# Two-layer hybrid decoder trunk: the first layer's normalised input from a column-wise copy of x instead of from transposes

## The chip, the cores and the metric

One core of one Trainium2 chip. Its engines are TensorE (PE, matrix products; PEld is its loading of weights), VectorE (DVE), ScalarE (ACT) and GpSimd (POOL); SyncE (SP) issues most DMA loads. The metric is device microseconds (us) of one execution, the median of several runs.

## The reference

Two layers of a decoder trunk, 256 positions, width 1024, float32. What matters here is how each layer begins, and what runs beside it:

```python
for l in range(DEPTH):                                  # DEPTH = 2
    h = rms_norm(x, norm_g[l])                          # x * rsqrt(mean(x*x) + eps) * g, per position
    proj = h @ w_in[l]                                  # 1024 -> 5120 columns
    q_a, k_a, v_a, q_h, f_h, i_h, q_m, z = split(proj)
    o_a = causal attention of 8 heads (QK norm, partial rotary) on q_a, k_a, v_a
    o_h = rms_norm(gated linear recurrence(q_h, f_h, i_h))
    kv_m = rms_norm(mem, mem_norm_g[l]) @ w_mem_kv[l]   # 256 memory tokens, 1024 -> 1024 columns
    o_m = attention of q_m on kv_m
    y = concatenate([o_a, o_h, o_m]) * silu(z)
    x = x + y @ w_out[l]
```

## The kernel before

**Precision.** Every large product is done as three: each operand is split in a high part (a cast to the format fp32r) and the remainder, so that the weights are `wh` and `wl`, the normalised input `hTh` and `hTl` (both in the tile `hT`, 8 blocks k of 128 columns, each with 256 positions high and 256 low), the memory tokens `mTh` and `mTl`.

**Weights.** All weights come in chunks of 128x1024 float32 (512 KB) through four buffers `wr`, loaded by SP in the order of use: 8 of `w_mem_kv`, 40 of `w_in`, 12 of `w_out`, and again for the second layer. ACT casts a chunk to `wh` (L201, or L205 where a gain is multiplied in) and DVE subtracts to get `wl` (L215, L219); each has three buffers. PE's products are at L262 (`mm`) and L266 (`mm_row`, kept in program order).

**Order.** The program is written as a main line of matmul groups; between their parts it steps generators (`g_norm`, `g_km`, `g_mem_r`, ...) that issue the other work. From this a scheduler makes one fixed list of instructions for each engine, which the engine works in order; what is marked with `keep_in_program_order` isn't moved.

**The first stage.** The main line begins with `group_kv`, the product of the memory tokens with `w_mem_kv`, chunks c0 to c7; its key half is finished first, then its value half. The memory tokens come already as columns (`mem_t`, put so on the host), and rows of them (`memr`) come as well, only for the squares of their norm (`g_mem_r`, L442 on ACT); the factor `rm` is applied after the product. `g_km` copies the key half out of PSUM (`kn`, L624 on DVE for one half of the positions and L625 on ACT for the other) and goes on to its norm (`sq`, `ssk`, `rk`).

**The layer's input.** Beside that product `g_norm(0)` makes `hT` from the rows `xs`: squares on ACT (L459), the factor `r` (`msx` on DVE, `rx` on POOL), two scalings `xn` on DVE (L467), 16 transposes of 128x128 on PE (L475, a product with the unit matrix `ident`) into four PSUM tiles `sd`, and from there eight times a cast with the gain on ACT (L483, 128x256) and a subtraction on DVE (L484). Then comes `group_a`, whose first products (the forget gate) read `wh` and `hT`, both parts of one k at a time, in the order of k. `g_norm(1)` does the same for the second layer.

Of the kernel before, what the change touches and what calls it, by code (L numbers as in the profile page):

```python
# [22 lines left out]
D = 1024  # L23
# [22 lines left out]
def hymba_kernel(ctx: ExitStack, tc: tile.TileContext, x, mem, mem_t, positions, w_in, w_out, w_mem_kv,  # L46
# [17 lines left out]
    def room(what, n=1):  # L64
        while held[what] + n > room_of[what]:
            yield
# [97 lines left out]
    def load(dst, src):  # L164
        tc.keep_in_program_order(nc.sync.dma_start(dst, src))
# [211 lines left out]
    dma_to(8)  # L377
    for t in range(2):
        load(memr[t], dram(mem, t * 128 * D, [[D, 128], [1, D]]))
# [74 lines left out]
    def g_norm(l):  # L454
# [11 lines left out]
        for t in range(2):  # L466
            nc.vector.tensor_scalar(xn[t], xs[:, t], r[:, t:t + 1], None, op0=OP.mult)  # L467
        yield 3
        for kp in range(4):
            yield from room("sd")  # L470
            pt = side_tile()
            for j in range(2):
                k = kp * 2 + j
                for t in range(2):
                    ins = nc.tensor.transpose(pt[:, j * 256 + t * 128:j * 256 + (t + 1) * 128],  # L475
                                              xn[t][:, k * 128:(k + 1) * 128], ident)
                    if l == 0:
                        tc.keep_in_program_order(ins)
            for j in range(2):
                k = kp * 2 + j  # L480
                c = GR_NORM + 8 * l + k
                src = pt[:, j * 256:(j + 1) * 256]
                nc.scalar.activation(hTh[:, k], src, AF.Copy, scale=gT[:, c:c + 1])  # L483
                nc.vector.scalar_tensor_tensor(hTl[:, k], in0=src, scalar=gT[:, c:c + 1],  # L484
                                               in1=hTh[:, k].bitcast(F32), op0=OP.mult, op1=OP.subtract)
            rel()
            if kp % 2 == 1:
                yield
# [110 lines left out]
    for tag, n, bufs in (("PTh", 1792, 1), ("PTl", 1792, 1), ("hX", 512, 1), ("qk", 1024, 1), ("sq", 512, 2),  # L599
                         ("vmh", 1024, 1), ("vml", 1024, 1), ("kmh", 1024, 1), ("kml", 1024, 1), ("as", 512, 2),  # L600
                         ("al", 256, 2), ("hF", 1024, 1), ("sg", 512, 2), ("ih", 1024, 1),
                         *((f"y{c}{br}", 1024, 1) for br in (H_, A_, M_) for c in "hl"), ("hT1", 512, 1), ("blk", 1536, 1)):
# [156 lines left out]
    def y_tiles(br):  # L759
        if f"y{br}" not in T:  # L760
            T[f"y{br}"] = [sb.tile([128, 4, 256], F32R, name=f"y{c}{br}", tag=f"y{c}{br}", bufs=1) for c in "hl"]
        return T[f"y{br}"]
# [595 lines left out]
```

## Time and profile before

| what | value |
|---|---|
| runs | 391.07 to 391.2 us, median 391.19 us (3 runs) |
| profiled execution | span 389.4 us from its first to its last instruction; no time of its own is given beside it |
| PE busy | 383.4 us (98%), mean granted clock 0.999 |
| DVE / ACT / POOL busy | 320.7 / 247.8 / 84.4 us |
| bytes moved | 84.48 MB, mean 217 GB/s |
| all transposes to `hT`, both layers (L475) | 32 instructions |

The time of a run is about 1.8 us above the span, for what lies around the program. A PE matmul record shows its latency too, so that records overlap; the distance from start to start is what one costs. The kernel's stage in question lies between about 14 us, when the squares of x begin, and 36 us, when the first two chunks of `w_in` are used up.

### The profile page before, as it was taken

What the parts mean: (1) busy time and instruction counts of PE and PEld (TensorE: products, weight loads), DVE (VectorE), ACT (ScalarE), POOL (GpSimd) and SP (SyncE); (2) the same over time, 40 slices, a digit from 0 to 9 for tenths busy, and PEclk for the clock granted to TensorE, in tenths of its full rate; (3) what the DMA queues carried; (4) which work ended last, traced back from release to release, by engine and by line L of the source; (5) the groups of instructions that cost most, each with busy time, mean ns of one, the idle gap of its engine ahead of it and who ended that gap; (6) DMA issues with size and microseconds to landing.
All of it is one profiled execution on the core that took longest, in us unless ns stands there. A gap on an engine that the chain in (4) does not pass through costs nothing.

```text
span 389.4 us, 6794 instructions
## 1 busy us (share of the span) xinstructions
PE 383.4 (98%) x2455; PEld 319.5 (82%) x2455; DVE 320.7 (82%) x621; ACT 247.8 (64%) x414; POOL 84.4 (22%) x129
## 2 busy tenths in 40 slices
PE   8999999999999999999999999999999999999996
PEld 5888888788788888778888888888888888877885
DVE  4789899999659999967577689899696799997663
ACT  5988755567768849464375756445765984885540
POOL 3004400534102522500000040014061063152000
PEclk9999999999999999999999999999999999999999
DMA  7986595539534889985464568636765179999512
GB/s 257 418 312 190 185 312 180 163 111 320 176 107 150 272 277 337 309 269 176 158 205 164 175 204 260 226 109 195 238 198 185 54 266 278 335 275 291 184 47 108
DMA packets 26241, 84.48 MB, mean 217 GB/s; under 512 B 3552, under 2 KB 5984, under 8 KB 26208
## 3 DMA queue, kind: packets, MB, share of 16 engines
q1 hardware_dynamic: 22304, 71.31, 54.5%
q0 software_dynamic: 3616, 12.59, 10.7%
q8 instruction: 19, 0.31, 0.3%
q10 hardware_dynamic: 288, 0.15, 0.1%
q14 instruction: 14, 0.11, 0.1%
HBM read 74.60 MB, written 9.44 MB: 216 GB/s over the span
## 4 chain that ended last, share of the span: by engine, by line
PE 90%; DVE 3%; DMA 3%; ACT 2%; issue 1%; SPq 0%; DVEq 0%; ACTq 0%
PE acc L262 62%; PE acc L1244 17%; PE sd L262 5%; PE sd L266 4%; DMA wr<-in_w_out_dram 2%; DMA wr<-in_w_mem_kv_dram 1%; ACT P L1169 1%; PE sd L475 1%; ACT wh L201 1%; DVE wl L215 1%; DVE wl L219 1%; DVE blk L1185 1%; DVE yl L186 1%; PE sd L1000 0%; PE sd L1130 0%
## 5 line engine op out<-in xcount | busy, mean ns | idle before, releaser
L201 ACT CAST wh<-wr 128x1024 fp32r<-128x1024 f32 x96 | 100.7, 1050 | 69.3 <-PE acc L262 49.3
L215 DVE TENSOR_TENSOR wl<-wr,wh 128x1024 fp32r<-128x1024 f32 x96 | 117.0, 1219 | 26.3 <-ACT wh L201 26.1
L262 PE MATMUL acc<-wh,hT 128*128 128x512 f32 x384 | 122.9, 394 | 0.0
L262 PEld LDWEIGHTS acc<-wh,hT 128*128 128x128 f32 x384 | 71.5, 188 | 15.8 <-issue 0.7
L262 PE MATMUL acc<-wl,hT 128*128 128x512 f32 x192 | 75.6, 394 | 0.0
L262 PE MATMUL acc<-hT,wh 128*128 128x512 f32 x256 | 64.7, 392 | 0.0
L262 PEld LDWEIGHTS acc<-hT,wh 128*128 128x128 f32 x256 | 46.0, 189 | 8.4 <-ACT kn L625 0.4
L262 PEld LDWEIGHTS acc<-wl,hT 128*128 128x128 f32 x192 | 36.1, 188 | 7.3
L219 DVE SCALAR_TENSOR_TENSOR wl<-wr,gT,wh 128x1024 fp32r<-128x1024 f32 (+1 forms) x29 | 31.1, 1097 | 10.2 <-ACT wh L205 10.1
L1244 PE MATMUL acc<-wl,yh 128*128 128x512 f32 (+1 forms) x96 | 37.4, 390 | 0.7 <-DVE wl L219 0.7
L1244 PE MATMUL acc<-wh,yl 128*128 128x512 f32 (+1 forms) x96 | 37.2, 388 | 0.0
L262 PEld LDWEIGHTS acc<-hT,wl 128*128 128x128 f32 x256 | 34.9, 190 | 2.5
L205 ACT ACTIVATE wh<-wr,gT 128x1024 fp32r<-128x1024 f32 (+1 forms) x29 | 28.3, 1000 | 13.4 <-PE acc L1244 5.2
L262 PE MATMUL acc<-hT,wl 128*128 128x256 f32 x256 | 35.7, 282 | 0.0
L1244 PE MATMUL acc<-wh,yh 128*128 128x512 f32 (+1 forms) x96 | 33.1, 392 | 0.0
L262 PE MATMUL acc<-wh,mTh 128*128 128x512 f32 x64 | 25.5, 402 | 0.7 <-ACT wh L205 0.4
L262 PE MATMUL acc<-wh,mTl 128*128 128x512 f32 x64 | 25.0, 394 | 0.0
L965 POOL TENSOR_TENSOR rka<-msa,pw 128x8 f32<-128x8 f32 x4 | 9.9, 2477 | 58.2 <-DVE msa L964 58.2
L1051 ACT ACTIVATE P<-P,nba,rq 128x128 f32<-128x128 f32 (+1 forms) x32 | 17.1, 535 | 8.3 <-DVE nba L1045 8.3
L1244 PEld LDWEIGHTS acc<-wl,yh 128*128 128x128 f32 x96 | 18.0, 188 | 4.8 <-DVE wl L219 1.3
L1244 PEld LDWEIGHTS acc<-wh,yh 128*128 128x128 f32 x96 | 18.0, 188 | 4.2 <-issue 0.7
L1244 PEld LDWEIGHTS acc<-wh,yl 128*128 128x128 f32 x96 | 18.0, 188 | 3.6
(219 smaller groups left out, 589.0 us busy)
## 6 DMA issues: line engine op xcount, KB each, us to landing
wr<-in_w_in_dram SPq DMA_DIRECT2D x80, 512.0 KB, 4.1
wr<-in_w_out_dram SPq DMA_DIRECT2D x24, 512.0 KB, 5.2
wr<-in_w_mem_kv_dram SPq DMA_DIRECT2D x15, 512.0 KB, 4.3
there<-blk POOLq DMA_DIRECT2D x4, 768.0 KB, 6.3
PT<-there POOLq DMA_DIRECT2D x16, 192.0 KB, 4.6
there<-blk POOLq DMA_DIRECT2D x6, 512.0 KB, 5.2
there<-blk SPq DMA_DIRECT2D x4, 512.0 KB, 2.9
P<-there POOLq DMA_DIRECT2D x16, 128.0 KB, 6.5
```

The source lines that it names most:

```text
L186: T["DVE"] = nc.vector.tensor_tensor(lo, a, h.bitcast(F32), op=OP.subtract)
L201: nc.scalar.copy(whs[i], raws[i])
L205: nc.scalar.activation(whs[i][:, sl], raws[i][:, sl], AF.Copy, scale=gT[:, g:g + 1])
L215: nc.vector.tensor_tensor(wls[i], raws[i], whs[i].bitcast(F32), op=OP.subtract)
L219: ins = nc.vector.scalar_tensor_tensor(wls[i][:, sl], in0=raws[i][:, sl], scalar=gT[:, g:g + 1], in1=whs[i][:, sl].bitcast(F32), op0=OP.mu ...
L262: nc.tensor.matmul(o, lhsT=a, rhs=b, start=s, stop=e)
L266: tc.keep_in_program_order(nc.tensor.matmul(o, lhsT=a, rhs=b, start=s, stop=e))
L475: ins = nc.tensor.transpose(pt[:, j * 256 + t * 128:j * 256 + (t + 1) * 128], xn[t][:, k * 128:(k + 1) * 128], ident)
L965: nc.gpsimd.tensor_tensor(r[:, t8], ms[:, t8], pw[:, :8], op=OP.pow)
L1051: nc.scalar.activation(P[:, i, kc[t]], P[:, i, kc[t]], AF.Exp, bias=nb[:, c:c + 1], scale=rq[:, r:r + 1], accum_out=sm[:, c:c + 1])
L1169: T["exp"] = nc.scalar.activation(P[:, t, i], ps[t][:, i * 256:(i + 1) * 256], AF.Exp, bias=nb[:, c:c + 1], scale=r[:, cr:cr + 1], accum_o ...
L1244: ins = nc.tensor.matmul(a, lhsT=y, rhs=wt[:, cs], start=n == (0 if to is None else nk - 2) and j == 0, stop=n == nk - 1 and j == 2)
```

## The change

The host hands over x a second time, as `x_t`: 128 partitions are the 128 columns of a block, and along them stand 8 strips of 32 positions with the 8 blocks k in each. Two loads of 512 KB bring it into the tile `xT` on SP's queue, ahead of those of `memr`. In the first layer `g_norm` now leaves out `xn` and the transposes. It copies the factor `r` of each position across 128 columns (`rc`, DVE); two products of `rc` with `ident` put the factors of all 256 positions on every partition (`rb`, PSUM); eight instructions on DVE scale `xT` by gain and factor in place; and for each half of the k, ACT casts 128x1024 to `hTh` and DVE subtracts 128x1024 to `hTl`. `xT` shares its place with the recurrence's output tiles, which become one tile for that. The second layer is as before.

```diff
+    xT = sb.tile([128, 8, 8, 32], F32, name="xT", tag=f"y{H_}", bufs=1)
+    for t in range(2):
+        load(xT[:, 4 * t:4 * t + 4].rearrange("p q k i -> p (q k i)"),
+             dram(x_t, t * 128 * D, [[D, 128], [1, D]]))
     for t in range(2):
         load(memr[t], dram(mem, t * 128 * D, [[D, 128], [1, D]]))
...
         nc.gpsimd.tensor_tensor(r, ms, pw[:, :2], op=OP.pow)
         yield
-        for t in range(2):
-            nc.vector.tensor_scalar(xn[t], xs[:, t], r[:, t:t + 1], None, op0=OP.mult)
-        yield 3
-        for kp in range(4):
...
+        if l == 0:
+            rc = sb.tile([128, 2, 128], F32, name="rc", tag="sq", bufs=2)
+            nc.vector.tensor_copy(rc, r[:, :, None].to_broadcast([128, 2, 128]))
+            yield 2
+            rb = side_tile()
+            for t in range(2):
+                mm_row(rb[:, t * 128:(t + 1) * 128], rc[:, t], ident)
+            rb3 = rb[:, :256].rearrange("p (q i) -> p q i", i=32)
+            yield
+            for k in range(8):
                 c = GR_NORM + 8 * l + k
-                src = pt[:, j * 256:(j + 1) * 256]
-                nc.scalar.activation(hTh[:, k], src, AF.Copy, scale=gT[:, c:c + 1])
-                nc.vector.scalar_tensor_tensor(hTl[:, k], in0=src, scalar=gT[:, c:c + 1],
-                                               in1=hTh[:, k].bitcast(F32), op0=OP.mult, op1=OP.subtract)
+                nc.vector.scalar_tensor_tensor(xT[:, :, k], in0=xT[:, :, k], scalar=gT[:, c:c + 1], in1=rb3,
+                                               op0=OP.mult, op1=OP.mult)
+                if k % 4 == 3:
+                    ks = slice(k - 3, k + 1)
+                    src = xT[:, :, ks].rearrange("p q k i -> p k q i")
+                    hi, lo = (a[:, ks].rearrange("p k (q i) -> p k q i", i=32) for a in (hTh, hTl))
+                    nc.scalar.copy(hi, src)
+                    nc.vector.tensor_tensor(lo, src, hi.bitcast(F32), op=OP.subtract)
+                    yield
             rel()
...
+    def strips(a):
+        return a.reshape(2, 4, 32, 8, 128).transpose(0, 4, 1, 3, 2)
```

The lists of the engines change with it. ACT's list before, from the last squares of the memory tokens to the casts of the first chunks of `w_in` (`wh<-wr`, L201):

```order
L483 ACTIVATE hT<-sd,gT 128x256 x3
L442 ACTIVATE memr,ssm<-memr 128x1024
L483 ACTIVATE hT<-sd,gT 128x256 x3
L201 CAST wh<-wr 128x1024
L483 ACTIVATE hT<-sd,gT 128x256 x2
L201 CAST wh<-wr 128x1024
L625 COPY kn<-acc 128x512
L665 ACTIVATE vmh<-acc,rm 128x512
```

And now, from the first half of `hT` on (the first square of `memr` stands just ahead in both lists):

```order
L487 CAST hT<-xT 128x4x256
L446 ACTIVATE memr,ssm<-memr 128x1024
L649 COPY kn<-acc 128x512
L487 CAST hT<-xT 128x4x256
L635 ACTIVATE sq<-kn 128x512
L201 CAST wh<-wr 128x1024
L635 ACTIVATE sq<-kn 128x512
L201 CAST wh<-wr 128x1024
```

The first cast of `w_in` has moved from ahead of `kn` to behind `kn`, the last of `hT` and the first `sq`.

DVE's list before, from the last three remainders of the memory weights to the first of `w_in`:

```order
L219 SCALAR_TENSOR_TENSOR wl<-wr,gT,wh 128x1024 x3
L484 SCALAR_TENSOR_TENSOR hT<-sd,gT,hT 128x256 x3
L445 TENSOR_SCALAR msm<-ssm 128x2
L448 RECIPROCAL rm_159<-msm 128x2
L449 TENSOR_SCALAR rm_159<-rm_159 128x2
L484 SCALAR_TENSOR_TENSOR hT<-sd,gT,hT 128x256 x3
L215 TENSOR_TENSOR wl<-wr,wh 128x1024
L624 COPY kn<-acc 128x512
```

And now:

```order
L219 SCALAR_TENSOR_TENSOR wl<-wr,gT,wh 128x1024 x3
L481 SCALAR_TENSOR_TENSOR xT<-xT,gT,sd 128x8x32 x8
L648 COPY kn<-acc 128x512
L488 TENSOR_TENSOR hT<-xT,hT 128x4x256
L449 TENSOR_SCALAR msm<-ssm 128x2
L452 RECIPROCAL rm_162<-msm 128x2
L453 TENSOR_SCALAR rm_162<-rm_162 128x2
L488 TENSOR_TENSOR hT<-xT,hT 128x4x256
L636 TENSOR_REDUCE ssk<-sq 128x4
L215 TENSOR_TENSOR wl<-wr,wh 128x1024
```

`kn` now stands ahead of both subtractions of `hT`, and a reduction over `sq` ahead of the first remainder of `w_in`. On PE the two products of `rc` stand ahead of chunk c5, where the 16 transposes stood in two groups near its end; further on, in the first half of the first layer, small instructions of the rotary tables and the recurrence change places with their neighbours on DVE and ACT, and POOL's lists differ in one place (four copies for the rotary tables, behind the masks now).

More of the change, by code (lines that the diff above doesn't have):

```diff
@@ L45, in hymba_kernel @@
 @with_exitstack
-def hymba_kernel(ctx: ExitStack, tc: tile.TileContext, x, mem, mem_t, positions, w_in, w_out, w_mem_kv,
+def hymba_kernel(ctx: ExitStack, tc: tile.TileContext, x, x_t, mem, mem_t, positions, w_in, w_out, w_mem_kv,
                  gains, moba_g, out):
@@ L465, in g_norm @@
         yield
[L466 to L488 removed]
+        if l == 0:
[8 more added lines that the diff above has]
+            for k in range(8):
+                c = GR_NORM + 8 * l + k
+                nc.vector.scalar_tensor_tensor(xT[:, :, k], in0=xT[:, :, k], scalar=gT[:, c:c + 1], in1=rb3,
[7 more added lines that the diff above has]
+                    yield
+            rel()
+        else:
+            for t in range(2):
+                nc.vector.tensor_scalar(xn[t], xs[:, t], r[:, t:t + 1], None, op0=OP.mult)
+            yield 3
+            for kp in range(4):
+                yield from room("sd")
+                pt = side_tile()
+                for j in range(2):
+                    k = kp * 2 + j
+                    for t in range(2):
+                        nc.tensor.transpose(pt[:, j * 256 + t * 128:j * 256 + (t + 1) * 128],
+                                            xn[t][:, k * 128:(k + 1) * 128], ident)
+                for j in range(2):
+                    k = kp * 2 + j
+                    c = GR_NORM + 8 * l + k
+                    src = pt[:, j * 256:(j + 1) * 256]
+                    nc.scalar.activation(hTh[:, k], src, AF.Copy, scale=gT[:, c:c + 1])
+                    nc.vector.scalar_tensor_tensor(hTl[:, k], in0=src, scalar=gT[:, c:c + 1],
+                                                   in1=hTh[:, k].bitcast(F32), op0=OP.mult, op1=OP.subtract)
+                rel()
+                if kp % 2 == 1:
+                    yield
@@ L760, in y_tiles @@
         if f"y{br}" not in T:
-            T[f"y{br}"] = [sb.tile([128, 4, 256], F32R, name=f"y{c}{br}", tag=f"y{c}{br}", bufs=1) for c in "hl"]
+            if br == H_:
+                y = sb.tile([128, 2, 4, 256], F32R, name=f"y{br}", tag=f"y{br}", bufs=1)
+                T[f"y{br}"] = [y[:, 0], y[:, 1]]
+            else:
+                T[f"y{br}"] = [sb.tile([128, 4, 256], F32R, name=f"y{c}{br}", tag=f"y{c}{br}", bufs=1) for c in "hl"]
         return T[f"y{br}"]
@@ L1339 @@
     laid = {
-        "x": v["x"], "mem": v["mem"], "mem_t": columns(v["mem"]).reshape(128, 4, 512).transpose(1, 0, 2),
+        "x": v["x"], "x_t": strips(v["x"]), "mem": v["mem"], "mem_t": columns(v["mem"]).reshape(128, 4, 512).transpose(1, 0, 2),
         "positions": v["positions"].reshape(2, 128).T,
```

2 lines of the change are left out of this document (1 added, 1 removed).

## The prediction

> **What bounds the kernel now.** I read first the page's totals and its slices, then who TensorE (PE) waits for, then the chain of work that ended last, and last the order of time on each engine from 12 to 48 us, where the change lies.
>
> ```profile
> span 389.4 us, 6794 instructions
> PE 383.4 (98%) x2455; PEld 319.5 (82%) x2455; DVE 320.7 (82%) x621; ACT 247.8 (64%) x414; POOL 84.4 (22%) x129
> PE   8999999999999999999999999999999999999996
> PE 90%; DVE 3%; DMA 3%; ACT 2%; issue 1%; SPq 0%; DVEq 0%; ACTq 0%
> PE acc L1244 <- DVE wl L219: 0.7, 2, 0.3
> PE acc L262 <- ACT wh L205: 0.4, 1, 0.4
> ```
>
> PE is busy in 383.4 of 389.4 us, and the two last rows (us waited in all, times, longest) are, beside start-up, all that it waits for: 0.4 us at the first weights, and 0.35 us at the head of each output projection. So PE bounds every stage after the first 8 us, its work is done in a fixed order, and a microsecond of PE work that goes, goes from the end too, unless PE now has to wait where it didn't. The span is the profiled execution's 389.4 us; the median of the runs is 391.19, 1.8 us more for what lies around the span, which I carry over.
>
> The stage in question is the memory product (eight weight chunks, c0 to c7), behind which the first layer's input product starts. Rows of the chain, then two of PE's own order of time (start, duration; a duration has a matmul's latency in it, the pitch is the distance of starts):
>
> ```profile
> 22.72 0.87 PE sd L475 x8
> 23.59 0.46 PE acc L262 x2
> 24.05 0.87 PE sd L475 x8
> 92.35 0.89 PE sd L262 x8
> ...
> 20.28 0.39 PE L262 MATMUL acc<-wh,mTh 128*128 128x512 f32 x1
> 30.25 3.57 PE L262 MATMUL acc<-hT,wh 128*128 128x512 f32 x15
> ```
>
> Chunk c5 starts at 20.28 and the first product that reads hT at 30.25; between them lie 36 matmuls and the 16 transposes, without a gap. hT was never waited for.
>
> **The change on PE.** The 16 transposes go: 2 x 0.87 = 1.74 us. Two float32 products of 128x128 come. Their price is the row at 92.35: four such products are recorded as 8 instructions and take 0.89 us, 0.22 each, so 0.44 us. They stand behind c4, at 20.28; what they read, rc, is ready earlier (below). Net -1.30 us: 36 matmuls take 30.25 - 20.28 - 1.74 = 8.23 us, so PE is done with the memory product at 20.28 + 0.44 + 8.23 = 28.95 instead of 30.25. That is all the change can give, if hT and the first input weights (wh of the forget gate's first chunk) are there at 28.95. The question is whether they are.
>
> **The two new loads.** x_t is 1 MiB in two loads, put on SP's queue ahead of the two loads of memr and of all the loads of w_in. Issue to landing of the last memory weights, of memr and of the first w_in chunk, each from the rows of its own moment, and the queue's rate:
>
> ```profile
> L165 SPq DMA_DIRECT2D wr<-in_w_mem_kv_dram x1: 327/327/327, 14.8 to 14.8; - x1
> DMA to landing us min/median/max: 5.2/5.2/5.2
> L165 SPq DMA_DIRECT2D memr<-in_mem_dram x2: 423/424/424, 15.1 to 15.6; - x2
> DMA to landing us min/median/max: 6.1/6.4/6.8
> L165 SPq DMA_DIRECT2D wr<-in_w_in_dram x1: 328/328/328, 17.2 to 17.2; - x1
> DMA to landing us min/median/max: 6.4/6.4/6.4
> 15.00:17.50 2.50, 2.50 (x13) 2.07 (x12) 1.47 (x3) 2.38 (x4) 0.00 (x0) 1.00 1.04 415
> 27.50:30.00 2.50, 2.50 (x12) 2.06 (x11) 2.21 (x4) 2.50 (x5) 0.79 (x4) 1.00 0.14 45
> ```
>
> They land at 20.0, 21.2, 22.4 and 23.6: one 512 KB load every 1.2 us, at 415 GB/s with the 16 engines full (last two columns: DMA share, GB/s). So xT takes the places of memr, at 21.2 and 22.4; memr lands at 23.6 and 24.8, and the first w_in chunk at 26.0 instead of 23.6, the next at about 27.2. By 27.5 the queue has run dry in the kernel before (share 0.14), so the 2.4 us are made up there and later loads don't move.
>
> The Trainium skill ("DMA: Bandwidth & Descriptors", Queues, rings and completion order) says that completion is not in order of issue on one engine's queue, since a load may be spread over fewer of the DMA engines; here the four landings come in order and evenly, so the row decides; by the rule memr could land before xT, which is my first rival, worked out from rows below.
>
> **ACT, where the new wait is.** ACT works its list strictly in order:
>
> ```profile
> 17.56 3.62 ACT L205 ACTIVATE wh<-wr,gT 128x1024 fp32r<-128x1024 f32 x3 [0.15 <-DMA wr<-in_w_mem_kv_dram]
> 21.23 1.06 ACT L442 ACTIVATE memr<-memr 128x1024 f32<-128x1024 f32 x1
> 24.90 1.05 ACT L442 ACTIVATE memr<-memr 128x1024 f32<-128x1024 f32 x1
> 25.94 1.19 ACT L483 ACTIVATE hT<-sd,gT 128x256 fp32r<-128x256 f32 x3
> 27.01 1.06 ACT L201 CAST wh<-wr 128x1024 fp32r<-128x1024 f32 x1
> 27.95 0.86 ACT L483 ACTIVATE hT<-sd,gT 128x256 fp32r<-128x256 f32 x2
> 29.62 0.62 ACT L625 COPY kn<-acc 128x512 f32<-128x512 f32 x1
> 30.09 0.73 ACT L665 ACTIVATE vmh<-acc,rm 128x512 fp32r<-128x512 f32 x1
> 32.19 1.19 ACT L611 ACTIVATE sq<-kn 128x512 f32<-128x512 f32 x2
> L185 ACT CAST yh<-zh 128x512 fp32r<-128x512 f32 x4 | 2.3, 613 | 0.0
> ```
>
> Pitches from it: a square of memr 1.04 (24.90 to 25.94), a 1024-wide cast 0.94 (27.01 to 27.95), the copy kn 0.47 (29.62 to 30.09), a square sq about 0.57 (two in 1.19, overlapped). The last row is a cast through a strided pattern: 613 ns, no dearer than the plain 512-wide kn, so I price the two hT casts as plain. Before, the first w_in cast ran at 27.01, with only two of the eight hT pieces behind it, and was done 2.2 us ahead of need. In the changed list it stands behind memr, hT cast, memr, kn, hT cast and sq, and the first of these now waits for memr until 23.6 while ACT, done at 21.2, idles 2.4 us. From there: 23.65 + 1.04 = 24.69, hT cast to 25.63, memr (landed 24.8) to 26.67, kn to 27.14, hT cast to 28.08, sq to 28.65, wh 1.06 to 29.71. PE, free at 28.95, starts at 29.75: it waits 0.8 us. Against 30.25 that leaves -0.5 us.
>
> **DVE, which must keep up.** The rows:
>
> ```profile
> 17.70 0.72 POOL L464 TENSOR_TENSOR rx<-msx,pw 128x2 f32<-128x2 f32 x1 [13.84 <-DVE msx L463]
> 18.45 1.42 DVE L467 TENSOR_SCALAR xn<-xs,rx 128x1024 f32<-128x1024 f32 x2 [0.84 <-POOL rx L464]
> 19.79 3.67 DVE L219 SCALAR_TENSOR_TENSOR wl<-wr,gT,wh 128x1024 fp32r<-128x1024 f32 x3
> 26.07 0.17 DVE L445 TENSOR_SCALAR msm<-ssm 128x2 f32<-128x2 f32 x1 [0.55 <-ACT memr L442]
> 26.55 1.26 DVE L484 SCALAR_TENSOR_TENSOR hT<-sd,gT,hT 128x256 fp32r<-128x256 f32 x3
> 28.10 1.22 DVE L215 TENSOR_TENSOR wl<-wr,wh 128x1024 fp32r<-128x1024 f32 x1 [0.29 <-ACT wh L201]
> 29.24 0.68 DVE L624 COPY kn<-acc 128x512 f32<-128x512 f32 x1
> 42.43 1.50 DVE L642 TENSOR_TENSOR kn<-kn,rk 128x512 f32<-128x512 f32 x2 [1.81 <-POOL rk L639]
> ```
>
> Two xn scalings (1.42) go; the copy rc comes at 18.45, between 0.17 (the two-wide row) and 0.42 us (a 256-wide product); I take 0.3, so rc is there at 18.75, and the products at 20.28 wait for nothing. The three wl follow until 22.4, just when xT has landed. The eight scalings of xT have the old 256-wide form, 1.26 / 3 = 0.42 each (strided in and out; their bounds are this and 0.68, the price of a 512-wide row): the fourth is done at 24.1, half a microsecond before ACT's first hT cast wants it, the eighth at 25.8. Then kn waits for PE's key half: 20.28 + 0.44 + 24 x 0.229 + 0.17 of latency = 26.4, to 27.0; the first hT remainder, a 1024-wide subtraction as at 28.10, to 28.2; three small ones (26.07 to 26.55) to 28.7; the second remainder to 29.8. PE asks for the first four k at 29.75, for the others 0.9 us later: both are there. The first wl of w_in follows a reduction at 30.4 and is done at 31.6, wanted after 16 matmuls at 33.4; the second at 33.5, wanted at 34.4. So DVE does not decide, with 0.8 us to spare at the narrowest. DVE has 0.3 + 2 x 1.15 - 1.42 = 1.2 us more to do; what takes it up is the idle 1.81 us at 42.43, where it waited for POOL's rk, which starts earlier now since the sums for it come before the second wl. If that cover were too small, DVE is 98% busy from 60 to 90 us and its remainders would come late: rival 3.
>
> **Sum.** -1.74 + 0.44 + 0.8 = -0.5 us: 391.19 - 0.5 = 390.7 us, 0.13% faster. What a measurement of this kernel can tell from no change is about 0.2%, 0.78 us, so this is no difference that counts. The bounds of the unknown prices: all eight scalings at 0.68 would put the fourth at 25.1 and move the chain 0.45 later, -0.05; a memr landing 0.3 either way moves it as much.
>
> **Rivals.**
> 1. ACT gets there sooner, so that more of the 1.30 us stays. If memr landed before xT, at 21.2 and 22.4 as now, ACT's first hT cast would wait for the fourth scaling at 24.1, and everything would run 0.5 earlier, until kn: that can't start before 26.4. From there 0.47 + 0.94 + 0.57 + 1.06 puts wh at 29.44. PE then gains 0.8 us: 390.4, at the edge of 0.2%. The full 1.30 (389.9) needs ACT's pitches a tenth shorter as well, or one of the two 0.35 us waits at the output projections to vanish on the way. For it: five of the six pitches are taken where ACT was crowded; against: the landings are in order.
> 2. Slower than before: the loads ahead of memr stretch. The decisive point is its landing: past 24.2 instead of 23.6 the 0.5 us are gone, past 25.0 the kernel is 0.2% slower; 25.5 gives 392.1. For it: the added load sits in the one stretch where the queue is full, and every later step on ACT hangs on it; against: four equal steps of 1.2 us.
> 3. DVE, with 1.2 us more to do and little idle time from 48 to 92 us, hands on a late remainder of a weight chunk in that stretch: 0.5 us taken back, 391.2, no change at all. Against: the 1.81 us, and that no PE wait on wl shows there now.
>
> **How the numbers follow.** My forecast, -0.2 to -0.78: 0.47. Rival 3, also within 0.2%: 0.09. Rival 1, past 0.78: 0.32, since its price ends at the edge and two small things can push it over. Rival 2: 0.12, all of it counted slower. So faster 0.32, same 0.56, slower 0.12. The range runs from the full gain, 389.9, to the first half of rival 2, 391.6; the likeliest case's own is 390.4 to 391.0.
>
> **What would show it.** In the changed kernel's order of time: two rb products in 0.44 us behind c4; memr's first square at about 23.6 with ACT idle 2.4 us before it, released by a load; PE idle some 0.8 us before its first product on hT, released by ACT's cast wh, at about 29.75; the w_in chunks landing 2.4 us later, then no trace of it past 35 us. I am wrong if PE doesn't wait there (full gain), if it waits past 30.25, or if a wait on wl shows between 48 and 92 us.

## The result, and the profile after

The changed kernel takes 393.76 us (median of 5 runs, 392.62 to 394.21) against 391.07 for the kernel before (5 runs, 390.47 to 391.20): ratio 1.0063, 95% interval 1.0048 to 1.0078. It is slower by 0.6% (the two medians stand 2.7 us apart); I had forecast 0.5 us faster. The profiled execution of the changed kernel is one of 393.76 us with a span of 392.0 us, that of before had a span of 389.4: the two profiles stand 2.6 us apart, and these 2.6 us are what has to be found.

The page's totals, and rows from the list of what TensorE (PE) waited for, after the change:

```profile
PE 382.8 (98%) x2443; PEld 318.1 (81%) x2443; DVE 321.8 (82%) x622; ACT 247.0 (63%) x408; POOL 87.7 (22%) x129
PE acc L262 <- ACT wh L201: 2.6, 1, 2.6
PE acc L262 <- DVE wl L215: 0.6, 1, 0.6
PE acc L262 <- ACT ih L753: 0.3, 1, 0.3
```

Three waits are new: one of 2.6 us for the cast of the first `w_in` chunk, where I had 0.8, and two near 80 us, for `wl` and `ih`, that I had not. Where they stand, in PE's order of time (start, duration; idle time and its releaser in brackets), with the products that spread the norm's factor and the four last matmuls of the memory product:

```profile
20.23 0.60 PE L266 MATMUL sd<-ident,rc 128*128 128x128 f32 x4
20.59 0.48 PE L262 MATMUL acc<-wh,mTh 128*128 128x512 f32 x1
...
27.94 1.07 PE L262 MATMUL acc<-wl,mTh 128*128 128x512 f32 x4
31.64 3.94 PE L262 MATMUL acc<-hT,wh 128*128 128x512 f32 x16 [2.63 <-ACT wh L201]
...
78.03 0.89 PE L266 MATMUL sd<-hQ,hK 128*32 128x48 f32 x64
79.23 0.50 PE L262 MATMUL acc<-wh,hT 128*128 128x512 f32 x1 [0.31 <-ACT ih L753]
81.67 0.50 PE L262 MATMUL acc<-wl,hT 128*128 128x512 f32 x1 [0.56 <-DVE wl L215]
87.59 0.46 PE L266 MATMUL sd<-hQ,hK 128*32 128x32 f32 x32
```

The products `sd<-hQ,hK` belong to the gated recurrence; I call each block of them an HGRN group and use the third and the fourth of the first layer as marks in time. The same two in the kernel before:

```profile
76.52 0.89 PE L266 MATMUL sd<-hQ,hK 128*32 128x48 f32 x64
84.82 0.46 PE L266 MATMUL sd<-hQ,hK 128*32 128x32 f32 x32
```

The first product on hT starts at 31.64, before at 30.25: +1.39 us. From the third HGRN group to the fourth it is 87.59 - 78.03 = 9.56 us, before 84.82 - 76.52 = 8.30, with the same 32 large products between: +1.26. Together 2.65 us, the difference of the spans. Everywhere else the two kernels run side by side, to within 0.2 us. (An idle time of 0.56 us costs 0.7 in starts, since the matmuls ahead of it no longer overlap with those behind.)

The first loss, on ACT and on VectorE (DVE):

```profile
23.62 1.06 ACT L446 ACTIVATE memr<-memr 128x1024 f32<-128x1024 f32 x1 [2.52 <-DMA memr<-in_mem_dram]
24.67 1.04 ACT L487 CAST hT<-xT 128x1024 fp32r<-128x1024 f32 x1
25.61 1.05 ACT L446 ACTIVATE memr<-memr 128x1024 f32<-128x1024 f32 x1
28.59 0.59 ACT L649 COPY kn<-acc 128x512 f32<-128x512 f32 x1 [1.84 <-PE acc L262]
29.08 1.05 ACT L487 CAST hT<-xT 128x1024 fp32r<-128x1024 f32 x1
30.02 0.63 ACT L635 ACTIVATE sq<-kn 128x512 f32<-128x512 f32 x1
30.55 1.03 ACT L201 CAST wh<-wr 128x1024 fp32r<-128x1024 f32 x1
28.37 0.69 DVE L648 COPY kn<-acc 128x512 f32<-128x512 f32 x1 [2.68 <-PE acc L262]
```

Up to the end of memr's second square, at 26.7, every row stands within 0.1 us of the prediction. Then ACT has `kn` next in its list, and `kn` waits 1.84 us for the key half of the memory product; the second hT cast, the square and the cast of the first weight chunk are queued behind it. The reason is in PE's list. The last rows of the memory product before, where the key half's two accumulators are `acc_199` and `acc_200`:

```
L262 MATMUL acc_199<-wl_322,mTh_140 128x512
L262 MATMUL acc_200<-wl_322,mTh_140 128x512
L262 MATMUL acc_201<-wh_294,mTh_140 128x512
L262 MATMUL acc_201<-wh_294,mTl_141 128x512
L262 MATMUL acc_201<-wl_322,mTh_140 128x512
L262 MATMUL acc_202<-wh_294,mTh_140 128x512
L262 MATMUL acc_202<-wh_294,mTl_141 128x512
L262 MATMUL acc_202<-wl_322,mTh_140 128x512
```

and after, where they are `acc_201` and `acc_202`:

```
L262 MATMUL acc_203<-wh_296,mTh_143 128x512
L262 MATMUL acc_203<-wh_296,mTl_144 128x512
L262 MATMUL acc_204<-wh_296,mTh_143 128x512
L262 MATMUL acc_204<-wh_296,mTl_144 128x512
L262 MATMUL acc_201<-wl_324,mTh_143 128x512
L262 MATMUL acc_202<-wl_324,mTh_143 128x512
L262 MATMUL acc_203<-wl_324,mTh_143 128x512
L262 MATMUL acc_204<-wl_324,mTh_143 128x512
```

In the changed list both halves of the last two chunks run interleaved, and the key half ends two matmuls from the end. I had counted 24 matmuls up to its end, behind the place where chunk c5 begins; that is the order in which the program writes them, and not that of either list. Even before, it ended behind 30 of the 36, as the first of these two lists shows. An estimate with 30 in place of 24 moves `kn` from 26.67 to 27.76 and, with the prediction's own chain behind it, PE's start from 29.75 to 30.84: by before's list already the change would have come out 0.6 us slower, not 0.5 faster.

The second loss, ACT's rows after:

```profile
76.23 1.28 ACT L579 ACT_TABLE_LOAD   x1
77.53 0.23 ACT L579 ACTIVATE sc<-rt 128x32 f32<-128x32 f32 x1
77.67 1.03 ACT L201 CAST wh<-wr 128x1024 fp32r<-128x1024 f32 x1
78.60 0.58 ACT L753 COPY ih<-acc 128x512 f32<-128x512 f32 x1
```

and before:

```profile
74.22 1.05 ACT L201 CAST wh<-wr 128x1024 fp32r<-128x1024 f32 x1
75.28 1.28 ACT L555 ACT_TABLE_LOAD   x1
76.71 0.57 ACT L729 COPY ih<-acc 128x512 f32<-128x512 f32 x1
```

Sin with its table load (the rotary tables, nothing that the change touches) has moved ahead of the cast of chunk 17 of the projections. On DVE the two products `kr`, which wait for Sin, have moved ahead of that chunk's remainder in the same way. After, and then before:

```profile
77.79 0.17 DVE L581 TENSOR_SCALAR rt<-sc 128x16 f32<-128x16 f32 x1 [0.58 <-ACT sc L579]
78.27 1.29 DVE L996 TENSOR_TENSOR kr<-acc,rtA 128x512 f32<-128x512 f32 x2 [0.30 <-POOL rtA L591]
80.41 1.21 DVE L215 TENSOR_TENSOR wl<-wr,wh 128x1024 fp32r<-128x1024 f32 x1
```

```profile
76.09 1.21 DVE L215 TENSOR_TENSOR wl<-wr,wh 128x1024 fp32r<-128x1024 f32 x1
77.62 1.29 DVE L968 TENSOR_TENSOR kr<-acc,rtA 128x512 f32<-128x512 f32 x2 [0.18 <-POOL rtA L567]
```

In the changed kernel the remainder is done at 81.6, and PE waits for it until 81.67; the copies `ih`, which free accumulators, come later by the same order. The Trainium skill ("ScalarE activation tables: per-element evaluation and per-set limits", What a function is on this engine) puts a table load at 1283 ns; the rows of both kernels have 1.28 us, so the load isn't dearer than before, it stands in another place.

### The profile page after: what moved, and what is told of

It reads as the page before. It is cut to its first block, busy times and chain, and to the rows that moved or that the text cites. A ratio compares the mean times of both kernels' runs of the same rounds, so it can differ in the third digit from the quotient of the medians.

```text
span 392.0 us, 6764 instructions
## 1 busy us (share of the span) xinstructions
PE 382.8 (98%) x2443; PEld 318.1 (81%) x2443; DVE 321.8 (82%) x622; ACT 247.0 (63%) x408; POOL 87.7 (22%) x129
## 4 chain that ended last, share of the span: by engine, by line
PE 89%; ACT 4%; DVE 4%; DMA 1%; issue 1%; SPq 0%; POOL 0%; DVEq 0%; ACTq 0%
PE acc L262 62%; PE acc L1272 17%; PE sd L262 5%; PE sd L266 4%; ACT P L1197 2%; DMA wr<-in_w_mem_kv_dram 1%; ACT wh L201 1%; DVE wl L215 1%; DVE wl L219 1%; ACT L777 1%; DVE blk L1213 1%; DVE y L186 1%; PE sd L1028 0%; PE sd L1158 0%; PE sd L501 0%
## 5 line engine op out<-in xcount | busy, mean ns | idle before, releaser
L201 ACT CAST wh<-wr 128x1024 fp32r<-128x1024 f32 x96 | 100.6, 1049 | 69.0 <-PE acc L262 41.2
L215 DVE TENSOR_TENSOR wl<-wr,wh 128x1024 fp32r<-128x1024 f32 x96 | 116.7, 1217 | 26.4 <-ACT wh L201 26.2
L219 DVE SCALAR_TENSOR_TENSOR wl<-wr,gT,wh 128x1024 fp32r<-128x1024 f32 (+1 forms) x29 | 31.1, 1096 | 10.4 <-ACT wh L205 10.3
L1272 PE MATMUL acc<-wh,yl 128*128 128x512 f32 (+1 forms) x64 | 24.7, 386 | 0.0
L1272 PE MATMUL acc<-wl,yh 128*128 128x512 f32 (+1 forms) x64 | 24.7, 386 | 0.0
L993 POOL TENSOR_TENSOR rka<-msa,pw 128x8 f32<-128x8 f32 x4 | 10.8, 2712 | 59.8 <-DVE msa L992 59.8
L1272 PE MATMUL acc<-wh,yh 128*128 128x512 f32 (+1 forms) x64 | 21.8, 386 | 0.0
L1272 PE MATMUL acc<-wh,y 128*128 128x512 f32 x64 | 20.9, 398 | 0.0
L262 PE MATMUL acc<-wl,mTh 128*128 128x512 f32 x64 | 19.5, 390 | 0.0
L993 POOL TENSOR_TENSOR rqa<-msa,pw 128x8 f32<-128x8 f32 x4 | 12.0, 3001 | 30.7 <-DVE msa L992 30.7
```

The costliest lines, as they stand in the source:

```text
L201: nc.scalar.copy(whs[i], raws[i])
L215: nc.vector.tensor_tensor(wls[i], raws[i], whs[i].bitcast(F32), op=OP.subtract)
L219: ins = nc.vector.scalar_tensor_tensor(wls[i][:, sl], in0=raws[i][:, sl], scalar=gT[:, g:g + 1], in1=whs[i][:, sl].bitcast(F32), op0=OP.mu ...
L262: nc.tensor.matmul(o, lhsT=a, rhs=b, start=s, stop=e)
L993: nc.gpsimd.tensor_tensor(r[:, t8], ms[:, t8], pw[:, :8], op=OP.pow)
L1272: ins = nc.tensor.matmul(a, lhsT=y, rhs=wt[:, cs], start=n == (0 if to is None else nk - 2) and j == 0, stop=n == nk - 1 and j == 2)
```

## The experiments

All of them are the changed kernel with small edits, but for one of the kernel before. Two names in the edits: `issue_after(x)` puts an instruction behind x in its engine's list, and `mm_row` pins matmuls in the order written. Positions in time differ between profiles, ahead of every edit: the place where c5 begins before, or the two products of `rc` now, lies at 20.28 before, at 20.23 in the changed kernel, and between 19.09 and 22.35 in the kernels below, in part since PE's first products wait for the first weights and memory columns between nothing and 1.9 us. So I compare waits and distances, and where I give a position beside that of the kernel before, I say how far apart the two stood at this place. The times in the heads are medians, with the kernel before on the same chip beside them.

**The key half first (392.52 against 391.18; ratio 1.0030, 1.0013 to 1.0048).**

```diff
-                mm(acc[g][t], th[:, c, ts], wH, c == 0, False)
...
+                m = mm_row if c >= 6 and c0 == 0 else mm
+                m(acc[g][t], th[:, c, ts], wH, c == 0, False)
...
-        nc.scalar.copy(kn[:, 1], acc[1])
+        with tc.issue_after(T["sq"].ins):
+            nc.scalar.copy(kn[:, 1], acc[1])
```

(`T["sq"]` is memr's second square; the other two products of each chunk are pinned in the same way.)

> The changed kernel, with the last two chunks of the memory product pinned on TensorE so that the key half of both comes ahead of the value half, and the ACT copy of kn held behind the second square of memr; the rows of ACT, DVE and POOL stay as they were, word for word. Theory (the place of the key half's end): in the changed kernel kn on ACT began at 28.59 us, since the key half's last product stood two matmuls from the end of the list; now that half ends 12 matmuls (2.75 us) earlier, kn begins at about 26.65, behind memr, and TensorE's first product with hT at about 29.7 in place of 31.64. The later loss near 80 us stays. Time 393.76 - 1.9 = 391.9 us (391.5 to 392.3). Rival A (the two added loads hold the chain): the start of kn moves, but the start on hT stays within 0.3 us of 31.64, and the time within 0.3 of 393.8. Rival B (VectorE is behind): TensorE starts at 29.7, waits longer for wl before 62 us, the first HGRN group stands at 62.9 as before, time 393.5 or more.

ACT and PE of this kernel:

```profile
24.30 1.06 ACT L447 ACTIVATE memr<-memr 128x1024 f32<-128x1024 f32 x1 [3.43 <-DMA memr<-in_mem_dram]
27.34 0.56 ACT L651 COPY kn<-acc 128x512 f32<-128x512 f32 x1
30.37 3.93 PE L262 MATMUL acc<-hT,wh 128*128 128x512 f32 x16 [2.07 <-ACT wh L201]
79.98 0.50 PE L262 MATMUL acc<-wl,hT 128*128 128x512 f32 x1 [0.53 <-DVE wl L215]
```

`kn` no longer waits: it follows memr at once. The chain from memr's start to `kn`'s is 27.34 - 24.30 = 3.04 us (3.02 predicted), and to PE's start 6.07 (6.10 predicted). So ACT's pitches and its order were right, and the list of PE was the fault. But the start came 1.27 us earlier, not 1.9, because memr landed 0.68 later than in the first profile. Issue to landing of memr's loads in the changed kernel and in this one:

```profile
DMA to landing us min/median/max: 7.6/8.1/8.5
```

```profile
DMA to landing us min/median/max: 8.5/8.9/9.3
```

Over the thirteen profiles with the two added loads the median landing was 8.0 to 8.2 us in five and 8.8 to 9.4 in eight (before: 6.4): my 2.4 us for memr's later landing held in the five; in this kernel memr's first load is issued 0.9 us later, counted from the last memory weights, and takes 2.5 more to land, 3.4 in all. The loss near 80 us stayed (9.12 us from the third group to the fourth; wait of 0.53), although PE came there 1.3 us earlier: it hangs on the order of rows there, not on how late the first layer starts.

**Sin early (395.14 against 391.18; ratio 1.0091, 1.0065 to 1.0116).**

```diff
-                with behind("ACT"):
+                with tc.issue_after(T["sin"].ins) if i == 20 else behind("ACT"):
                     nc.scalar.copy(whs[i], raws[i])
...
-        nc.scalar.activation(sc8, a2, AF.Sin)
+        T["sin"] = nc.scalar.activation(sc8, a2, AF.Sin)
```

> The changed kernel, with ACT's cast of one chunk of w_in (chunk 12 of the projections) held behind Sin, so that Sin and its table load stand two casts earlier in ACT's list, at about 64 us, and rtA and kr follow earlier on POOL and VectorE. The first 60 us are untouched. Theory (the order of the small things at 76 to 82 us): in the changed kernel the table load and Sin (1.5 us) stood ahead of the cast of chunk 17, and two products kr behind Sin ahead of its wl; out of that place they cost TensorE nothing, and about 1.2 us come back: the first HGRN group stays at 62.9, that at 87.7 comes to 86.4, time 392.5 us (392.1 to 393.0). Rival (the 1.25 us are VectorE's added work of the first 30 us, which comes due here): the waits for wl stay or move, and the time stays at 393.4 to 394.0.

```profile
66.09 0.73 PE L262 MATMUL acc<-wh,hT 128*128 128x512 f32 x2 [0.64 <-ACT wh L201]
68.34 0.50 PE L262 MATMUL acc<-wl,hT 128*128 128x512 f32 x1 [1.51 <-DVE wl L215]
```

The waits at 79 and 82 us are gone, and two larger ones stand at 66 and 68: the rotary rows that Sin needs have come ahead of a remainder on DVE. My sum was wrong; the rival that the waits move was right, and understated. Between 60 and 90 us DVE is busy 29.3 of 30 us in the kernel before: any row that is put forward there pushes a remainder back.

**Both edits (393.09; ratio 1.0049, 1.0029 to 1.0069).**

> Both edits at once, the key half first and Sin early. Theory: the two losses are separate and add up: 393.76 - 1.9 - 1.2 = 390.7 us (390.2 to 391.2), TensorE on hT at 29.7, the HGRN group of 87.7 at about 84.5. Rival (they are one loss: what comes earlier at 30 us runs into the same late engine): 391.5 to 392.5.

PE starts on hT at 31.32, with memr's first square only at 25.25, and waits 0.56 and 0.53 us at 66 and 68. The gain of the first edit is there (counted from the place of c5, where this profile stood 0.46 us later than the changed kernel's, the start comes 0.8 us earlier), the second costs; neither number of mine was met.

**`kn` behind the first weight cast (393.16; ratio 1.0051, 1.0030 to 1.0071).** PE's list is left as it was.

```diff
-        nc.scalar.copy(kn[:, 1], acc[1])
+        with tc.issue_after(T["c8"].ins) if l == 0 else nullcontext():
+            nc.scalar.copy(kn[:, 1], acc[1])
```

(`T["c8"]` is the cast of w_in's first chunk.)

> The changed kernel, with TensorE's list of the memory product as it is, but ACT's copy of kn held behind the cast of the first chunk of w_in, so that ACT goes from the second square of memr to hT's second cast and to that cast without waiting for the key half. Theory: ACT is through with memr at 26.65, hT's cast ends at about 28.1 and wh at 29.1; TensorE is free at about 28.9 and starts on hT at about 29.2 in place of 31.64, so the key half's place in the list costs nothing by itself, only what is queued behind its copy. Time 393.76 - 2.4 = 391.4 us (390.9 to 391.9) if the loss near 80 us stays. Rival (TensorE needs the accumulators that kn frees, or VectorE's wl is late next): TensorE starts at 29.2 but waits again before 36 us for an accumulator or wl, and the time is 392.5 or more.

```profile
29.88 4.17 PE L264 MATMUL acc<-hT,wh 128*128 128x512 f32 x16 [1.70 <-DVE rm L455]
79.28 0.50 PE L264 MATMUL acc<-wh,hT 128*128 128x512 f32 x1 [1.89 <-ACT ih L756]
```

The first wait shrinks by 0.9 us without the key half being any earlier (the row names DVE's `rm`, which ended within 0.05 us of ACT's cast at 29.83; the cast is what the product reads). The rest of it is memr, whose first square could begin only at 23.99, and one square `sq` that stood ahead of the cast. The copies `ih` now come 1.89 us late, though Sin isn't near. So in this profile the 0.9 us gained at the start are given back near 80 us, and my 391.4 us is missed.

**Before's order near 80 us (398.69 against 391.22; ratio 1.0176, 1.0148 to 1.0205).** Sin and its tables are written behind the masks, and kr and MoBA's start wait for them in the program.

```diff
-        nc.scalar.activation(sc8, a2, AF.Sin)
...
+        while "c25" not in T:
+            yield
+        with tc.issue_after(T["c25"].ins):
+            nc.scalar.activation(sc8, a2, AF.Sin)
```

(`T["c25"]` is the cast of chunk 17 of the projections.)

> The changed kernel, with Sin, rtA and rtB written later in the program and Sin held behind ACT's cast of chunk 17, and kr written after them. At the third HGRN group ACT's rows now read hQb, the cast of chunk 17, table load, Sin, ih, and VectorE's rows wl of chunk 17 ahead of kr, both word for word as in the kernel before; the first 60 us are as in the changed kernel; some rows of MoBA's softmax at 100 to 130 us move too. Theory (the order of these rows cost 1.26 us between the HGRN groups at 78.0 and 87.6): no wait of TensorE for ih or wl there, the stretch from the third to the fourth HGRN group 8.3 us as before in place of 9.56, time 393.76 - 1.2 = 392.5 us (392.1 to 393.0). Rival (VectorE is late there whatever its order, since its added work of the first 30 us comes due): the stretch stays above 9.1 us, or a wait of like size stands within 20 us behind it, and the time is 393.3 or more.

The third group and the fourth:

```profile
80.15 0.89 PE L267 MATMUL sd<-hQ,hK 128*32 128x48 f32 x64
88.63 0.46 PE L267 MATMUL sd<-hQ,hK 128*32 128x32 f32 x32
```

It is 8.48 us from one to the other, with a wait of 0.33 for `ih` and none for `wl`. But one large product of 0.23 us stands outside this stretch now (31 for 32), so that the pace of the kernel before would be 8.07: 0.41 us are still lost, and 0.85 of the 1.26 us came back. The total is 5 us worse all the same. In the profile 2.1 us of that stand ahead of c5, before any row that the edit moves (22.35 against 20.23: the first weights were waited for 1.88 us, and from 8.3 to 11.7 the granted clock was 0.50). And between 103 and 174 us the profile falls back by another 3.6 us against the kernel before. There MoBA's rows, which are written behind kr, have moved too, and PE waits 1.0 us for `as` and 0.4 each for `y` of ACT and of DVE (164 to 168); the list of waits shows no more, so that about half of the 3.6 us stays open.

As a repair this is a failure; as a test of the place it says what was asked.

**The same with the key half first (397.14; ratio 1.0146, 1.0119 to 1.0174).**

> The edits of key_half_first and sin_late together: the two places where the prediction's steps stand otherwise in the rows, put as the prediction had them, and nothing else. Theory (these two steps are the whole miss, but for memr, which in four later profiles landed 8.9 to 9.1 us after its issue and not 8.1): 393.76 - 1.3 - 1.2 = 391.2 us (390.7 to 391.8), TensorE on hT at about 30.3, no wait for ih or wl near 80 us. Rival (something else costs time all along): 392.2 or more.

From the third group to the fourth 8.06 us (78.05 to 86.11), with the same 31 large products and no wait: here the whole 1.26 us came back. PE starts on hT at 30.13. Then 2.0 us are lost waiting for MoBA's `y` on ACT at 163, and twice the granted clock was 0.50 for 3.4 us, from 30.1 and from 163.2, each time right behind a wait of 2 us; the first of these cost about 1.5 us up to the first HGRN group (30.13 to 62.82, against 31.64 to 62.81 in the changed kernel). Both steps of the miss are undone here, and the total doesn't show it: a total is no test where the edit moves other rows.

**memr and `kn` behind the first weight cast (391.99 against 391.22; ratio 1.0024, 0.9998 to 1.0050).**

```diff
+        while "c8" not in T:
+            yield
         for t in range(2):
-            nc.scalar.activation(memr[t], memr[t], AF.Square, accum_out=ss[:, t:t + 1])
+            with tc.issue_after(T["c8"].ins):
+                T["sq"] = nc.scalar.activation(memr[t], memr[t], AF.Square, accum_out=ss[:, t:t + 1])
```

(and the edit of `kn` above)

> The changed kernel, with both squares of memr and the copy of kn on ACT held behind the cast of the first chunk of w_in, so that ACT's list reads both hT casts, that cast, then memr twice, then kn; TensorE's memory product is as in the changed kernel. Theory (TensorE's start on hT hangs on nothing but ACT's queue: memr's landing and the key half's end are late, hT itself isn't): hT's casts end by about 27, the cast of w_in's chunk by about 28, TensorE starts at about 29.1, when VectorE's copy of kn has freed an accumulator, in place of 31.64: -2.5 us, time 391.3 us (390.8 to 391.8) with the loss near 80 us as it was. Rival A (the loads of xT or of w_in are what is late): the start moves by less than 1 us. Rival B (rm, vmh and the accumulators that they free become late): TensorE starts at 29.1 but waits for an accumulator before 45 us, time 392.3 or more.

```profile
28.63 2.24 PE L262 MATMUL acc<-hT,wh 128*128 128x512 f32 x8 [0.20 <-DVE kn L651]
36.21 2.14 PE L262 MATMUL acc<-hT,wh 128*128 128x512 f32 x8 [1.39 <-DVE vml L694]
```

The start loses 0.2 us and no more: hT and the first weights were in time all along, and only what ACT had queued ahead of them was late. Rival B's wait is there as well: `rm` is later now, `vmh` and `vml` free two accumulators later, and PE pays 1.39 us at 36; the time, 391.99, lies between my range and the rival's.

**That together with before's order near 80 us (397.44; ratio 1.0151, 1.0123 to 1.0179).**

> The two edits of memr_kn_last and sin_late together. Theory: the two losses are separate, 393.76 - 2.5 - 1.2 = 390.1 us (389.6 to 390.7), about 1 us under the kernel before, which is what the change's smaller TensorE work is worth (1.3 us) with no wait added. Rival (VectorE, 94 to 97 percent busy from 30 to 85 us in the kernel before, can't follow a TensorE that starts 1 us earlier than there): new waits for wl between 60 and 90 us, time 391.0 or more.

Start at 28.07 with a wait of 0.20, 0.97 for `vml`, none between 40 and 90 us; then the late MoBA rows again, 2.15 us for `mP` at 184.6 and 1.8 in all for `y` and `as` at 160 to 164. Behind the wait at 184.6 the granted clock was 0.50 once more, from 186.2 to 189.6. So the rival named (DVE can't follow before 90 us) is not what happened, and my total was missed by 7 us.

**vmh ahead of the squares of `kn` (391.80 against 391.07; ratio 1.0015, 0.9998 to 1.0033).** In this schedule, unpinned, Sin falls behind both copies of `ih`.

```diff
+        while l == 0 and "vm" not in T:
+            yield
...
+            with tc.issue_after(T["vmi"].ins) if l == 0 else nullcontext():
+                sumsq(ss[:, t * 4:t * 4 + 4], kn[:, t], 4)
...
-            nc.scalar.activation(vmh[:, t], acc[t], AF.Copy, scale=rm[:, t:t + 1])
+            T["vmi"] = nc.scalar.activation(vmh[:, t], acc[t], AF.Copy, scale=rm[:, t:t + 1])
```

> memr_kn_last with one more edit: the squares of kn on ACT held behind vmh, so that vmh and vml, which free two accumulators, come ahead of sq and ssk. In its list Sin stands, without a pin, behind the cast of chunk 17 and behind both copies of ih. Theory: TensorE starts on hT at 28.6 as in memr_kn_last; its wait of 1.39 us for vml at 36.2 goes, since vmh follows the casts of chunks 9 and 10 at about 32.0 and vml ends at about 34.4, before TensorE wants the accumulator; the stretch from the third to the fourth HGRN group has no wait for ih or wl. Time 391.99 - 1.4 - 0.5 = 390.1 us (389.6 to 390.6), under the kernel before by about 1.1 us, which is what the 1.3 us of TensorE work that the change takes out are worth once no wait is added. Rival (VectorE is full from 30 to 85 us and gives the time back): new waits for wl between 40 and 90 us, 391.0 or more.

The 1.39 us are gone, and there is no wait between 40 and 90 us. One of 0.82 us for `wl` stands at 125.9 in their place: the rival, 40 us further on than I had put it, and the time is in the rival's range, not in mine.

**memr's first square between the hT casts (391.22 against 391.07; ratio 1.0013, 0.9990 to 1.0035).** `issue_after` the first hT cast for t = 0, the rest as in the last kernel.

> vm_first with the first square of memr between the two hT casts on ACT, where ACT idled 0.5 us in memr_kn_last, and the second behind the cast of w_in's first chunk. Theory: rm is known about 1 us earlier, TensorE's start stays at 28.6 to 29.0 (ACT: hT's cast to 25.0, memr from its landing at 24.0 to 25.3 to about 26.3, hT's cast to 27.3, wh to 28.3), 390.1 us (389.6 to 390.8). Rival (memr's landing sets the start once more, since hT's second cast is queued behind it): start at 29.3 or later, time 0.5 us or more over that of vm_first.

PE starts at 28.27, and at the third HGRN group it stands 1.5 us ahead of the kernel before (75.00 against 76.52), but 0.98 us of that were there at the place of c5 already (19.30 against 20.28): the lead that the change gives is 0.5 us. Behind 126 us it stands only 0.5 us ahead, less than at c5: the lead is gone, and more. The median, 391.22, is above my range. ACT at 99 us and PE at 125, and then SP's longest wait between 84 and 104 (us in all, times, longest):

```profile
99.32 1.05 ACT L201 CAST wh<-wr 128x1024 fp32r<-128x1024 f32 x1 [1.83 <-DMA wr<-in_w_in_dram]
125.47 0.50 PE L262 MATMUL acc<-wl,hT 128*128 128x512 f32 x1 [0.79 <-DVE wl L215]
```

```profile
SPq L106 <- DVE blk L95: 10.3, 1, 10.3
```

SP issues the loads of `w_in`, and between them the transfers that turn kr. It stood 10.3 us at the first of these, until DVE's `blk` was there (6.7 in the kernel before), and the loads behind it went out late.

**kr's transfers issued by POOL (390.27 against 390.83; ratio 0.9992, 0.9975 to 1.0009).** The lists of PE, ACT and DVE are those of the last kernel, word for word.

```diff
-            yield from across(o.rearrange("p (q r) -> p q r", q=4), flat, 8)
+            yield from across(o.rearrange("p (q r) -> p q r", q=4), flat, 8, q=nc.gpsimd if l == 0 else None)
```

> memr_mid_vm with one thing more: the transfers that turn layer 0's kr (one to there, four to kT) are issued by POOL and no longer by SP, where w_in's loads are queued between and behind them; the rows of TensorE, ACT and VectorE stay word for word. Theory (in memr_mid_vm the lead of 1.5 us over the kernel before was given back at 99 us, where ACT's cast waits 1.83 us for a load of w_in that SP issues behind the kT transfers, and qT, the table load, sg and the whole MoBA chain on VectorE up to wl at 124 us are queued behind that cast): the load lands before ACT wants it, sg comes at about 101.4 in place of 102.65, TensorE's wait of 0.79 us for wl at 125 goes, time 391.2 - 1.0 = 390.2 us (389.7 to 390.7), about 0.2 percent under the kernel before. Rival A (the load waits for its buffer, which VectorE's wl frees, not for its place on SP): the wait for the load at 99 us stays at 1.5 us or more, time 391.0 to 391.4. Rival B (the wait goes but another queue gives the time back): no wait for the load at 99 us, and 390.9 or more.

The same cast, and then all that PE waits for in this kernel:

```profile
97.40 1.05 ACT L201 CAST wh<-wr 128x1024 fp32r<-128x1024 f32 x1 [1.66 <-PE acc L262]
```

```profile
PE sd L262 <- DVE dm L394: 1.0, 1, 1.0
PE acc L262 <- ACT mTh L420: 1.0, 1, 1.0
PE acc L1279 <- DVE wl L219: 0.7, 2, 0.4
PE acc L262 <- DVE kn L651: 0.2, 1, 0.2
```

The load is in time, the cast 1.9 us earlier, the wait at 125 is gone, and the median is the expected one. From 29 us to the first output projection PE has no wait in the list. The start on hT stands 1.77 us ahead of the kernel before (28.48 against 30.25), the wait at that projection 1.39 (157.35 against 158.74); but 0.77 us of both were there at the place of c5 (19.51 against 20.28). So the change leads by 1.0 us at the start and keeps 0.6 (the rest goes in waits too short for the list, before 35 us): about half of the 1.3 us of PE work that it takes out, and close to the 0.56 us between the medians. The intervals of the last two kernels overlap, so of the step between them the wait that went is shown, and the gain in time is not. Against the kernel before the ratio has come from 1.0063 to 0.9992; the median is 0.56 us lower, but the interval still holds 1, so a gain over the kernel before is not shown.

**The two loads alone, in the kernel before (392.21 against 391.07; ratio 1.0023, 1.0006 to 1.0040).**

```diff
+    xT = sb.tile([128, 8, 8, 32], F32, name="xT", tag=f"y{H_}", bufs=1)
+    for t in range(2):
+        load(xT[:, 4 * t:4 * t + 4].rearrange("p q k i -> p (q k i)"),
+             dram(x_t, t * 128 * D, [[D, 128], [1, D]]))
     for t in range(2):
         load(memr[t], dram(mem, t * 128 * D, [[D, 128], [1, D]]))
...
```

(The recurrence's output tiles become one tile here too, to give `xT` its place.)

> The kernel before with the change's two loads of xT (1 MiB) ahead of memr's, their data not used; nothing else of the change. ACT's list puts the first square of memr behind seven of the eight hT evictions, the second behind the eighth, and both ahead of kn and of the cast of w_in's first chunk. Theory (the loads themselves cost time, since memr lands behind them and ACT's queue waits there): memr's landing at about 24 in place of under 21.2, the cast of w_in's first chunk ends at about 29.5 to 30.5, TensorE's start on hT within 0.5 us of the 30.25 before or later by at most 1 us; time 391.2 to 392.2. Rival A (the loads are hidden): within 0.3 us of the kernel before. Rival B (loads delay the w_in chunks themselves): waits for wr between 30 and 45 us, over 392.5.

```profile
29.89 2.11 PE L262 MATMUL acc<-hT,wh 128*128 128x512 f32 x8 [0.26 <-ACT wh L201]
79.63 0.50 PE L262 MATMUL acc<-wl,hT 128*128 128x512 f32 x1 [0.30 <-DVE wl L215]
```

About 1 us slower, within what the theory allowed. Only a part is lost at the start on hT: counted from c5 it comes 0.41 us later (10.38 against 9.97), since this list has the hT evictions ahead of memr. Another 0.5 us go in small waits up to the first HGRN group (31.51 us from the start on hT, before 31.05), and 0.6 near 80 us, which the theory did not have (8.90 us from the third group to the fourth, a wait for `wl`). ACT's rows there read table load, Sin, cast of chunk 17, `ih`, as in the changed kernel: two unused loads are enough to turn the order of rows there.

## Why the prediction was wrong, step by step

- **PE's work.** Right: 16 transposes gone, and the two products took 0.36 us (20.23 to 20.59; 0.44 predicted). PE was through with the memory product at 28.85; 28.95 was predicted.
- **The loads.** Right for the profiled execution: memr's first square waited 2.52 us for its load and began at 23.62 (23.65 predicted). The prediction set the Trainium skill's rule that completion is not in order of issue ("DMA: Bandwidth & Descriptors", Queues, rings and completion order) against four even landings; here memr came behind xT in every profile, as the rows had it, and rival 1 did not happen. The spread of memr's landing was too small, though: I allowed 0.3 us either way, and from its issue the first load took 0.9 to 1.5 us longer in eight of the thirteen profiles. That is past rival 2's 24.2 in these eight, so the gain would have been lost in most profiles even with the rest as I thought; that the first profile was one of the five that fit was luck.
- **ACT's chain.** Right in order and pitch up to 26.67, and in its whole length once the key half came first (6.07 us measured, 6.10 predicted).
- **The step that failed: "Then kn waits for PE's key half: 20.28 + 0.44 + 24 x 0.229".** The 24 matmuls were counted in the program's order. In the changed list the key half ends behind 34 of the 36, and in the list of before behind 30; DVE's `kn` began at 28.37 in place of 26.4 and ACT's at 28.59 in place of 26.67. These 1.9 us went on unshortened through the second hT cast, the square and the weight cast: start at 31.64 in place of 29.75. One look at the accumulators' numbers in the list would have shown it. Key half first, and `kn` behind the cast, show it from two sides.
- **The second step that failed: the sum, "-1.74 + 0.44 + 0.8", has only terms of the first 30 us.** I took everything behind 35 us as unmoved, though the text on the change says that small instructions change places further on. The order near 80 us was another, and it cost 1.26 us. Rival 3 had the right engine, DVE, and the right stretch, 48 to 92 us, but the wrong cause (1.2 us of added work coming due) and 0.5 us as price. The profiles speak for the order as the cause: PE came 1.3 us earlier with the key half first and lost 0.8 us there all the same; with before's order put back 0.85 of 1.26 us returned, and all of it where the key half came first as well; and two unused loads in the kernel before brought the same order and a wait for `wl` there without any added work on DVE.
- **DVE's cover.** Half right. I said that POOL's `rk` starts earlier; it started at 40.76 (40.32 before), since four copies for the rotary tables came ahead of it, and the idle time in front of `kn` only shrank from 1.81 to 1.47 us. Nothing on PE came of it.
- **The sum.** The change of PE's work was right, the wait of 0.8 us was 2.79 in starts, and 1.26 were not in the sum: -1.74 + 0.36 + 2.79 + 1.26 = +2.67, against 2.6 between the spans.

Not settled: why memr lands after 8.1 us in some profiles and after 9 in others (the last section has a candidate), and whether the kernel with kr's transfers on POOL beats the kernel before.

## What to carry to other kernels

Where a scheduler sets the lists, read from the list itself at which row an accumulator is finished, and price every stretch whose order the comparison shows as changed, not only the one that the edit is about. On an engine that works in order, what is late is mostly what the late thing was queued behind: a start that waits is repaired by putting the row it needs ahead of rows that wait for something else, and that row's old neighbours are what waits next. And a total that moves the wrong way doesn't refute a theory about one place, if the edit moved other rows as well; measure the place.

## What the runs showed of the hardware that I had not expected

- Which engine issues a transfer mattered by 1.9 us for one load. The Trainium skill ("DMA: Bandwidth & Descriptors", Issuing engines are not separate DMA queues) says that spreading DMAs over several engines saves only the time to initiate them, which is usually small. Here five transfers moved from SP to POOL took away a 1.83 us wait for a load, since SP stood 10.3 us at one of them for its source, and every load behind it stood too.
- The same load, memr's first, in kernels whose first 15 us are alike, landed 7.6 us after issue in five profiles and 8.5 to 9.0 in eight. The traces have a candidate for it. In each of them one packet of 16 KB on the instruction queue (q8 in the profile), 0.88 to 0.97 us long, falls between 21 and 25 us. In the eight it begins within 0.25 us of xT's second landing, and memr follows that landing by 2.1 to 2.7 us in place of 1.2. In three of the five it begins as near, and memr's second load is the one that comes late, by 0.2 to 0.5 us; in the other two it begins later, at 24.2 and 24.4. No run moves this packet, so that it is the cause is not shown.
- Four times the granted clock was 0.50 for a stretch of 3.4 us: from 8.3, from 30.1 and 163.2, and from 186.2 us, in the three kernels that have before's order near 80 us (alone, with the key half first, and with memr and `kn` late). Each time a wait of PE of 1.9 to 2.2 us had ended at most 1.6 us before. Six other waits of 1.85 to 2.63 us, that of the changed kernel among them, were followed by no such stretch, so a wait of this length can cost more than itself but need not.
